# Moving one modulation group and issuing attention's value products in a row, in a two-layer hybrid diffusion backbone

## The chip, the cores and the metric

The kernel runs on one core of a Trainium2 chip. A core has five engines that run at once and are tied together by semaphores: TensorE (PE: matrix products; PEld is its weight loads), VectorE (DVE), ScalarE (ACT), GpSimd (POOL) and SyncE (SP), which here issues all the loads and stores. The metric is the device time of one execution in microseconds (us), as the median of several runs.

## The reference, cut to what matters

Two layers work on 512 latent and 256 context tokens of width 1024, in float32. Each layer has a mixer and a convolutional gated network (ConvFFN); in front of both stands an RMS norm whose scale and shift come from a conditioning vector, and behind both a gate from the same vector:

```python
def adaln_mods(cond, p):
    return jnp.split(jax.nn.silu(cond) @ p['ada_w'] + p['ada_b'], 6, axis=-1)

def trunk_layer(x_lat, x_ctx, c, c_ctx, p, mixer, rope, need_ctx):
    m_lat = [m[:, None, :] for m in adaln_mods(c, p)]
    m_ctx = adaln_mods(c_ctx, p)
    o_ctx, o_lat = mixer(modulate(x_ctx, p['norm_mix_g'], m_ctx[0], m_ctx[1]),
                         modulate(x_lat, p['norm_mix_g'], m_lat[0], m_lat[1]), p, rope, need_ctx)
    x_lat = x_lat + m_lat[2] * o_lat
    x_lat = x_lat + m_lat[5] * conv_ffn(modulate(x_lat, p['norm_ffn_g'], m_lat[3], m_lat[4]), p)
    ...
```

So a layer has six modulation groups of 1024 numbers for each of the two conditioning vectors: 0 and 1 are shift and scale of the mixer's norm, 2 its gate, 3 and 4 shift and scale of the network's norm, 5 the network's gate. Layer 1 needs the context's modulation for groups 0 and 1 only, since its context output is not used further.

Layer 0's mixer is latent attention beside RWKV-7 heads (a recurrence in chunks); layer 1's is Mamba-2 beside windowed attention. The windowed attention has 8 query heads in 2 groups; each block of 128 queries sees the 256 context keys and up to three blocks of 128 latent keys:

```python
s_win = jnp.where(mask, s_win, -jnp.inf)
p = sink_softmax(jnp.concatenate([s_ctx, s_win], axis=-1), sink).astype(v.dtype)
return (jnp.einsum('bghqk,bkgd->bqghd', p[..., :n_ctx], v_ctx)
        + jnp.einsum('bghqk,bkgd->bqghd', p[..., n_ctx:], vw))
```

## The kernel before, in words

Activations lie with the channels on the partitions, 128 at a time, and the tokens along the free dimension. Large products split weights and activations into a high and a low part in a reduced-width float (`whi`, `wlo`) and make three passes over them (`dense`, L367). `load_w` (L322) loads a weight, ScalarE makes the high part (L327), VectorE or GpSimd the low one (L328). All products go through the helper `mm` (L263), so they carry its line, L269, in the profile and are told apart by their tiles.

The order on each engine comes from a planner: it takes the instructions in the order of the program, simulates their times, and issues on each engine the earliest one of the program that is ready by its estimate. `tc.issue_after(ins)` puts what its block issues behind `ins` on the same engine. At run time each engine keeps its fixed order.

**Modulation.** A group is worked out in one of two ways.

- `ada_group` (L393), on TensorE: eight loads of 128 x 1024 weights (tile `aw`, 512 KB each), and for each four products `128*32 128x256` into four partition strips of one PSUM bank; a copy on VectorE (L406, `am`), two transposes (L409), and one addition of the bias that writes the group's columns of the tile `mods0` or `mods1` (L411).
- `ada_rows` (L415), on VectorE: the weights come transposed (`ada1t`), 128 outputs at a time, and one multiply with a running sum (L426) gives 128 outputs from a 128 x 1024 tile. It is a generator; each `next` makes one row. In the kernel before, it makes 16 rows for the context vector (groups 0 and 1 of layer 1) and 24 for the latent one (groups 0 to 2), 40 in all, and adds the bias at the end of each vector (L428).

Where the groups stand before: layer 0's groups 1 and 0 at the start (L520); layer 0's groups 2 to 5 in the mixer, one behind each of the four head pairs (p = 0 to 3) of the RWKV part (L802), with two weight buffers; layer 1's group 3 at the norm of layer 0's network, as the `fill` of `prenorm` (L1211), where TensorE waits for the norm; layer 1's rows during layer 0's network, two after each step j from 1 on (L1170); layer 1's group 4 behind layer 1's first norm (L1220) and group 5 in the fill at layer 1's network (L1630). In a fill, `paced` (L471) holds the products behind the last product before it.

**RWKV part of the mixer.** For each p, `features` (L613) projects and prepares, `rwkv_prep` (L716) makes the chunk products (`gk`), and `rwkv_inverse` (L755) inverts small triangular matrices, mostly on GpSimd (L765, L767), with transposes on VectorE (L759, L772 to L775) and products `iv`; its results go to memory and come back for the recurrence.

**Network.** `ffn` (L1130) takes 22 steps j in four groups (6, 6, 5, 5 steps in layer 0). A step makes two `up` products, each followed by a convolution (ScalarE L382, VectorE L383 and L385), a gate (L1163, L1164) and a split (L389, L390); behind each group come eight `down` products, each added to the residual with gate 5 (`resid`, L501). The rows are pinned behind the split's last instruction (`dve_last`).

**Windowed attention.** `swa_max` (L1481) works out the maxima of the scores of one query block, `swa_block` (L1516) its attention; block i + 1's maxima stand ahead of block i's attention in the program. In `swa_block`, for each block of 128 keys (4, 5, 5 and 4 of them for the four query blocks): for each of the 2 groups two score products and where needed a mask product into a PSUM tile `ab` (three buffers), one exponential on ScalarE (L1535) into `pt` (four buffers); then one value product for each group (L1538), `128*64 128x512`, group 0 into partitions 0 to 63 and group 1 into 64 to 127 of the tile `o`:

```python
            for g in range(2):
                mm(o[H[g]], lhsT=vv[:, tb * P + 64 * g:tb * P + 64 * g + 64], rhs=pts[g], start=n == 0,
                   stop=n == len(tbs) - 1)
```

GpSimd sums the exponentials (L1544). The output projection (`wo<-go`, from the Mamba part) needs none of this and is issued in between; the attention's part of it (`wo<-sh`, `wo<-sl`) follows.

Of the kernel before, what the change touches and what calls it, by code (L numbers as in the profile page):

```python
# [17 lines left out]
P = 128  # L18
D = 1024
# [3 lines left out]
NTOK = NCTX + NLAT  # L23
# [14 lines left out]
NAW = 2  # L38
# [90 lines left out]
def layout(inp):  # L129
    g = {k: np.asarray(v) for k, v in inp.items()}  # L130
    a = {}
    xt = np.concatenate([g["ctx"][0], g["x"][0]], 0).T
    a["xT"] = xt.reshape(KT, P, NTOK).transpose(1, 0, 2)
    cc = np.stack([g["c"][0], g["c_ctx"]], 1)
    a["cc"] = cc.reshape(KT, P, 2).transpose(1, 0, 2)
    a["ada"] = g["ada_w"].reshape(2, KT, P, 6, 1024).transpose(0, 3, 1, 2, 4)
    a["ada1t"] = g["ada_w"][1][:, :3 * D].T.reshape(24, P, D)
    a["ccrow"] = np.stack([g["c"][0], g["c_ctx"]], 0)
    ab = g["ab_w_in"][0]
    krs = np.concatenate([ab[:, 656:672], ab[:, 640:656]], 1)  # L140
    rw = ab[:, 672:]
    z64 = np.zeros((D, 64), np.float32)
    tiles = [rw[:, 1536:1600], ab[:, 640:672], krs, z64, rw[:, 1600:1664], rw[:, 1664:1792]]
    for p in range(4):
        for b in range(3):
            tiles.append(rw[:, b * 512 + p * P: b * 512 + (p + 1) * P])
    tiles.append(ab[:, :640])
    a["w_in"] = pack_w(np.concatenate(tiles, 1))
    qu = g["mla_w_q_up"][0].reshape(384, 8, 96)
    qu = np.concatenate([qu, qu[:, :, 80:96], qu[:, :, 64:80]], 2).reshape(384, 1024)  # L150
    a["w_q"] = pack_w(qu)
    kv = g["mla_w_kv_up"][0].reshape(256, 8, 128)
    a["w_k"] = pack_w(np.ascontiguousarray(kv[:, :, :64]).reshape(256, 512))
    a["w_v"] = np.ascontiguousarray(kv[:, :, 64:]).reshape(2, P, 4, P).transpose(1, 0, 2, 3).reshape(P, 8, P)
    a["w_out"] = pack_w(g["ab_w_out"][0])
    a["up"] = np.stack([pack_w(g["ffn_w_up"][i]) for i in range(2)])
    a["down"] = np.stack([pack_w(g["ffn_w_down"][i]) for i in range(2)])
    a["lora"] = np.concatenate([g["rwkv_w2"][0], g["rwkv_a2"][0]], 1).transpose(1, 0, 2)
    a["g2"] = g["rwkv_g2"][0]
    pv = {}  # L160
    for i in range(2):
        pv[f"ada_b{i}"] = g["ada_b"][i]
        pv[f"norm_mix_g{i}"] = g["norm_mix_g"][i]
        pv[f"norm_ffn_g{i}"] = g["norm_ffn_g"][i]
        for t in range(3):
            pv[f"conv_w{i}{t}"] = g["ffn_conv_w"][i, t]
        pv[f"conv_b{i}"] = g["ffn_conv_b"][i]
        pv[f"w0_{i}"] = g["rwkv_w0"][0, i]
        pv[f"a0_{i}"] = g["rwkv_a0"][0, i]
    pv["final_norm_g"] = g["final_norm_g"]  # L170
    pv["qn_g"], pv["kvn_g"] = g["mla_q_norm_g"][0], g["mla_kv_norm_g"][0]
    for n in ("mu_prev", "mu_next"):
        m = g["rwkv_" + n][0]
        z = np.zeros((64,), np.float32)
        q = [m[1536:1600], z, z, m[1600:1664], m[1664:1792]]
        for p in range(4):
            for b in range(3):
                q.append(m[b * 512 + p * P: b * 512 + (p + 1) * P])
        pv[n] = np.concatenate(q)
    for n in ("k_k", "k_a", "ln_g", "ln_b"):  # L180
        pv[n] = g["rwkv_" + n][0]
    pv["r_k"] = g["rwkv_r_k"][0].reshape(-1)
    for t in range(5):
        pv[f"sconv_w{t}"] = g["ssm_conv_w"][0, t]
    pv["sconv_b"] = g["ssm_conv_b"][0]
    pv["ssm_norm_g"] = g["ssm_norm_g"][0]
    pv["ssm_dx"] = np.repeat(g["ssm_d"][0], 64)
    z16 = np.zeros((16,), np.float32)
    for n in ("dt_bias", "a_log"):
        m = g["ssm_" + n][0]  # L190
        pv[n] = np.concatenate([m[0], z16, m[1], z16, np.zeros((64,), np.float32)])
    cd = g["cd_w_in"][0]
    zc, xc, dc, qc, kc, vc = np.split(cd, [1024, 2560, 2592, 3104, 3232], 1)
    qc = qc.reshape(D, 2, 4, 64).transpose(0, 2, 1, 3).reshape(D, 512)
    zp = np.zeros((D, 16), np.float32)
    dc = np.concatenate([dc[:, :16], zp, dc[:, 16:], zp, np.zeros((D, 64), np.float32)], 1)
    a["w_in1"] = pack_w(np.concatenate([xc, dc, zc, qc, kc, vc], 1))
    wo = g["cd_w_out"][0]
    wa = wo[1024:].reshape(2, 4, 64, D).transpose(1, 0, 2, 3).reshape(512, D)
    a["w_out1"] = pack_w(np.concatenate([wo[:1024], wa], 0))  # L200
    a["rows"] = g["swa_sink"][0].reshape(2, 4).T.reshape(1, 8)
    a["pv"] = np.concatenate([cols(np.asarray(pv[n], np.float32)) for n, _ in PV_SPEC], 1)
    cs = consts()
    a["const"] = np.concatenate([cs[n] for n, _ in CONST_ORDER], 1)
    a["scanm"] = cs["scanm"]
    a["scan2"] = cs["scan2"]
    a["const1"] = np.concatenate([cs["le"], cs["ge"]], 1)
    a["rope_a"], a["rope_c"], a["rope_s"] = rope_const()
    return {k: np.ascontiguousarray(v, dtype=np.float32) for k, v in a.items()}
# [3 lines left out]
def hybrid_kernel(ctx: ExitStack, tc: tile.TileContext, a, out):  # L213
# [201 lines left out]
    def ada_rows(mods, pool, bufs):  # L415

        for c in (1, 0):
            sr = T(pool, [P, D], "srow", 1)
            dma(sr, a["ccrow"][c:c + 1].partition_broadcast(P))
            act(sr, sr, AF.Silu)  # L420
            nt = 16 if c else 24
            for n in range(nt):
                w = T(pool, [P, D], "aw", bufs)
                dma(w, a["ada1t"][n])
                with tc.issue_after(dve_last[0]):
                    stt(out=w, in0=w, scalar=1.0, in1=sr, op0=ALU.mult, op1=ALU.mult, accum_out=mods[:, n, c:c + 1])  # L426
                yield
            tt(out=mods[:, :nt, c], in0=mods[:, :nt, c], in1=pv[:, PV["ada_b1"]:PV["ada_b1"] + nt], op=ALU.add)  # L428
# [367 lines left out]
    for p in range(4):  # L796
        fe = features(p)
        cur = rwkv_prep(p, *fe)
        if pend:
            rwkv_inverse(p - 1, *pend)  # L800
        pend = cur
        ada_group(0, p + 2, mods0, "pj", NAW)  # L802
    rwkv_inverse(3, *pend)
    close_pool("pp", "pa", "pj", "iv", "gk", "bkp")

# [166 lines left out]
    for tb in range(6):  # L972
        b = bank()
        n = 0
# [155 lines left out]
    def ffn(layer, mods, xs, segs, width, side, fill, nsegs=None, r=None, beside=None):  # L1130
# [13 lines left out]
        for gsz in FG[layer]:  # L1144
            us, ul = [], []
            halves = layer and j0 + gsz == FT
            for j in range(j0, j0 + gsz):
                cv = []
                for jj in (j, FT + j):
                    ps = acc()  # L1150
                    dense(ps, next_w("up"), P, hh, hl, segs=segs, by_pass=j < 2)
                    o = S()
                    conv3(o, ps, ALL, col(f"conv_w{layer}0", jj), col(f"conv_w{layer}1", jj), col(f"conv_w{layer}2", jj),
                          col(f"conv_b{layer}", jj), segs)
                    cv.append(o)
                    if halves:
                        raw = T("sb", [P, 8, P], "wraw", NWR)
                        dma(raw[:, :gsz], a["down"][layer, len(wb)][:, j0:])
                        hi, lo = [T("hold", [P, 4, P], "w", 16, F32R) for _ in range(2)]
                        split(hi, lo, raw[:, :gsz])  # L1160
                        wb.append((hi, lo))
                gt, vl = cv
                act(gt[:, n0:], gt[:, n0:], AF.Silu)  # L1163
                tt(out=vl[:, n0:], in0=gt[:, n0:], in1=vl[:, n0:], op=ALU.mult)  # L1164
                hi, lo = S(F32R), S(F32R)
                split(hi[:, n0:], lo[:, n0:], vl[:, n0:])
                us.append(hi)
                ul.append(lo)
                if beside is not None and j > 0:
                    next(beside, None)  # L1170
                    next(beside, None)
            if halves:
                break
            for m in range(8):
                ps = acc()
                dense(ps, next_w("down"), P, us, ul, nk=gsz, segs=segs)
                resid(xs[m], ps, mods, 5, m, segs)
            j0 += gsz
# [29 lines left out]
        close_pool("ffn")  # L1208

    open_pool("aw2", "right")  # L1210
    ffn(0, mods0, xs, SEG2, NTOK, "left", lambda: ada_group(1, 3, mods1, "aw2", 4),  # L1211
        beside=ada_rows(mods1, "aw2", 4))


# [301 lines left out]
    def swa_block(i, es):  # L1516
# [5 lines left out]
        for n, tb in enumerate(tbs):  # L1522
# [3 lines left out]
            for g in range(2):  # L1526
# [7 lines left out]
                pt = T("at2", [P, 512], "pt", 4)  # L1534
                act(pt, ps, AF.Exp)  # L1535
                pts.append(pt)
            for g in range(2):
                mm(o[H[g]], lhsT=vv[:, tb * P + 64 * g:tb * P + 64 * g + 64], rhs=pts[g], start=n == 0,  # L1538
                   stop=n == len(tbs) - 1)
            for g in range(2) if n < len(tbs) - (i == 3) else ():  # L1540
                if n == 0:
                    first[g] = pts[g]
# [105 lines left out]
```

## Time and profile before

| | |
|---|---|
| median of 3 runs | 2253.11 us (2247.74 to 2253.65) |
| the profiled execution | 2259.24 us, its span 2257.2 us, mean TensorE clock 0.955 |
| layer 0's mixer, up to the output projection | 0 to 732 us |
| output projection and norm | 732 to 821 us |
| layer 0's network | 821 to 1370 us |
| layer 1's mixer | 1370 to 1866 us, windowed attention from about 1700 on |
| layer 1's network | 1866 to 2257 us |
| modulation products: in the mixer's loop | 108 to 371 us |
| modulation products: fill at layer 0's network | 806 to 821 us |
| rows on VectorE (L426) | 40, from 854 to 1320 us |

How to read it. A line of the timeline has the start, the duration, the engine, the line, the operation, `output<-inputs`, the shape and a count of merged instructions; brackets hold the engine's idle time before it and what ended it. A float32 product with 128 x 512 moving elements takes two passes and shows as two records. A row of the table by stretch has, for each engine, its busy time and instruction count, then the granted TensorE clock (1.00 is full), the busy share of the DMA engines and GB/s. A line of the groups has the busy time and the mean duration in ns, then the idle time before. The chain that ended last is followed back from the last instruction, at each step to what released it.

### The profile page before, as it was taken

What the parts mean: (1) busy time and instruction counts of PE and PEld (TensorE: products, weight loads), DVE (VectorE), ACT (ScalarE), POOL (GpSimd) and SP (SyncE); (2) the same over time, 40 slices, a digit from 0 to 9 for tenths busy, and PEclk for the clock granted to TensorE, in tenths of its full rate; (3) what the DMA queues carried; (4) which work ended last, traced back from release to release, by engine and by line L of the source; (5) the groups of instructions that cost most, each with busy time, mean ns of one, the idle gap of its engine ahead of it and who ended that gap; (6) DMA issues with size and microseconds to landing.
All of it is one profiled execution on the core that took longest, in us unless ns stands there. A gap on an engine that the chain in (4) does not pass through costs nothing.

```text
span 2257.2 us, 33584 instructions
## 1 busy us (share of the span) xinstructions
PE 2066.3 (92%) x13360; PEld 1636.3 (72%) x13360; DVE 1393.8 (62%) x2157; ACT 930.8 (41%) x1437; POOL 506.2 (22%) x486
## 2 busy tenths in 40 slices
PE   5888989788998999999999999898878999999997
PEld 3666667576654878888888886776665667888886
DVE  5566865666877466456465554678984556554555
ACT  4445663532355253233132335644353345332434
POOL 0027686521233100000000014433631330000000
PEclk9989999698999999999999999998999999999998
DMA  8477777669521443333233333213426032323231
GB/s 300 121 202 197 192 204 192 213 175 294 168 96 54 152 140 114 102 103 119 87 115 101 103 112 117 90 47 117 133 85 159 28 126 71 94 89 98 84 117 61
DMA packets 183660, 292.00 MB, mean 129 GB/s; under 512 B 63616, under 2 KB 118944, under 8 KB 180432
## 3 DMA queue, kind: packets, MB, share of 16 engines
q1 hardware_dynamic: 183504, 289.86, 41.8%
q8 instruction: 105, 1.72, 0.3%
q14 instruction: 51, 0.42, 0.1%
HBM read 234.87 MB, written 47.33 MB: 125 GB/s over the span
## 4 chain that ended last, share of the span: by engine, by line
PE 64%; DVE 7%; ACT 5%; DMA 4%; issue 3%; POOL 1%; SPq 1%; DVEq 0%; ACTq 0%; POOLq 0%
PE acc L269 50%; PE sd L269 3%; PE b L269 3%; PE o L269 2%; PE ab L269 2%; PE wo L269 2%; DVE E L1376 2%; DMA E<-sp_ac 1%; PE ax L269 1%; POOL I L767 1%; DMA rec<-sp_rec 1%; POOL w L765 1%; ACT L433 0%; PE iv L269 0%; PE gk L269 0%
## 5 line engine op out<-in xcount | busy, mean ns | idle before, releaser
L269 PE MATMUL acc<-s,whi 128*128 128x512 f32 (+1 forms) x3104 | 766.6, 358 | 1.6 <-ACT s L480 1.6
L269 PEld LDWEIGHTS acc<-s,whi 128*128 128x128 f32 x3104 | 546.2, 188 | 93.9 <-ACT s L480 5.5
L269 PE MATMUL acc<-s,wlo 128*128 128x512 f32 (+1 forms) x1552 | 456.4, 354 | 0.0
L269 PE MATMUL acc<-h,whi 128*128 128x256 f32 (+2 forms) x1248 | 318.9, 369 | 18.6 <-DVE f L385 8.0
L327 ACT CAST whi<-wraw 128x1024 fp32r<-128x1024 f32 (+5 forms) x228 | 210.2, 923 | 278.3 <-PE acc L269 202.9
L269 PEld LDWEIGHTS acc<-s,wlo 128*128 128x128 f32 x1552 | 289.9, 188 | 47.1 <-DVE wlo L328 0.7
L269 PEld LDWEIGHTS acc<-h,whi 128*128 128x128 f32 (+1 forms) x1248 | 221.0, 195 | 71.4 <-issue 15.2
L328 DVE TENSOR_TENSOR wlo<-wraw,whi 128x1024 fp32r<-128x1024 f32 (+5 forms) x205 | 218.6, 1070 | 45.6 <-ACT whi L327 45.0
L383 DVE SCALAR_TENSOR_TENSOR s<-acc,pv,s 128x511 f32<-128x511 f32 (+1 forms) x132 | 87.0, 659 | 204.4 <-ACT s L382 204.0
L382 ACT ACTIVATE s<-acc,pv 128x512 f32<-128x512 f32 (+1 forms) x132 | 93.3, 707 | 234.8 <-PE acc L269 198.9
L501 DVE SCALAR_TENSOR_TENSOR x<-acc,mods,x 128x512 f32<-128x512 f32 (+1 forms) x136 | 79.4, 620 | 172.2 <-PE acc L269 172.1
L269 PE MATMUL acc<-h,wlo 128*128 128x256 f32 (+2 forms) x624 | 178.4, 360 | 0.0
L451 POOL TENSOR_TENSOR f<-f,f 128x768 f32<-128x768 f32 (+1 forms) x24 | 31.4, 1308 | 632.9 <-ACT f L446 623.0
L269 PEld LDWEIGHTS acc<-h,wlo 128*128 128x128 f32 (+1 forms) x624 | 118.4, 193 | 21.8 <-issue 5.5
L1194 POOL TENSOR_TENSOR s<-w,s 128x256 f32<-128x256 f32 x6 | 5.0, 861 | 382.9 <-ACT s L433 382.9
L385 DVE SCALAR_TENSOR_TENSOR s<-acc,pv,s 128x511 f32<-128x511 f32 (+1 forms) x132 | 87.0, 659 | 3.7
L767 POOL TENSOR_TENSOR I<-I,w 128x30 f32<-128x30 f32 (+14 forms) x120 | 77.4, 645 | 9.0
L765 POOL TENSOR_TENSOR w<-I 128x30 f32<-128x30 f32 (+14 forms) x120 | 68.9, 574 | 34.9 <-PE iv L269 26.0
L328 POOL TENSOR_TENSOR wlo<-wraw,whi 128x1024 fp32r<-128x1024 f32 x23 | 62.9, 2735 | 58.1 <-ACT whi L327 54.6
L389 ACT CAST s<-s 128x768 fp32r<-128x768 f32 (+1 forms) x44 | 32.0, 728 | 106.0 <-DVE s L1164 105.9
L1376 DVE TENSOR_SCALAR E<-E,acm 128x128 f32<-128x128 f32 x128 | 61.2, 547 | 15.0 <-ACT G L1373 15.0
L740 DVE TENSOR_TENSOR W<-gk,con 64x512 f32<-64x512 f32 x48 | 32.8, 683 | 53.5 <-ACT PB L739 50.7
(389 smaller groups left out, 3390.1 us busy)
## 6 DMA issues: line engine op xcount, KB each, us to landing
wraw<-up SPq DMA_DIRECT2D x88, 512.0 KB, 3.5
aw<-ada SPq DMA_DIRECT2D x72, 512.0 KB, 5.7
rec<-sp_rec SPq DMA_DIRECT2D x24, 1024.0 KB, 7.5
wraw<-w_in SPq DMA_DIRECT2D x47, 512.0 KB, 3.6
aw<-ada1t SPq DMA_DIRECT2D x40, 512.0 KB, 4.3
wraw<-down SPq DMA_DIRECT2D x40, 384.0 KB, 3.2
sp_rec<-tg SPq DMA_DIRECT2D x24, 384.0 KB, 3.2
E<-sp_ac SPq DMA_DIRECT2D x16, 512.0 KB, 6.1
```

Source lines behind the costliest of these rows:

```text
L269: ins = nc.tensor.matmul(o, lhsT=lhsT, rhs=rhs, start=start, stop=stop, skip_group_check=shared)
L327: nc.scalar.copy(hi[:, :kt], raw[:, :kt])
L328: (eng or tt)(out=lo[:, :kt], in0=raw[:, :kt], in1=hi[:, :kt].bitcast(F32), op=ALU.subtract)
L382: act(o[rows, t0:t0 + n], ps[rows, po:po + n], AF.Identity, scale=w1, bias=b)
L383: stt(out=o[rows, t0 + 1:t0 + n], in0=ps[rows, po:po + n - 1], scalar=w0, in1=o[rows, t0 + 1:t0 + n], op0=ALU.mult, op1=ALU.add)
L385: stt(out=o[rows, t0:t0 + n - 1], in0=ps[rows, po + 1:po + n], scalar=w2, in1=o[rows, t0:t0 + n - 1], op0=ALU.mult, op1=ALU.add)
L389: nc.scalar.copy(hi, src)
L501: stt(out=x[:, t0:t0 + n], in0=ps[:, po:po + n], scalar=mods[:, c6 * 8 + m, c:c + 1], in1=x[:, t0:t0 + n], op0=ALU.mult, op1=ALU.add)
L740: tt(out=w[hk], in0=b[hk].rearrange("p c (a t) -> p c a t", a=2), in1=mk[hk].rearrange("p (a t) -> p a t", a=2).unsqueeze(1).to_broadcast( ...
L765: eng.tensor_tensor(out=tmp, in0=I[:, m + 1:, m:m + 1].to_broadcast([P, n, m]), in1=I[:, m:m + 1, :m].to_broadcast([P, n, m]), op=ALU.mult)
L767: eng.tensor_tensor(out=I[:, m + 1:, :m], in0=I[:, m + 1:, :m], in1=tmp, op=ALU.add)
L1376: ts(out=e[:, h], in0=e[:, h], scalar1=acm[:, c, h0 + h:h0 + h + 1], scalar2=0.0, op0=ALU.subtract, op1=ALU.min)
```

## The change

Three things are changed.

- Layer 0's group 5, the last one in the mixer's loop (p = 3), is taken out there and becomes the fill at the norm of layer 0's network, in place of layer 1's group 3.
- Layer 1's group 3 goes to the rows on VectorE: the latent vector gets 32 rows in place of 24 (48 in all), the transposed weights grow to four groups, and the steps j of layer 0's network make two and three rows in turn (three in odd steps) in place of two.
- In the windowed attention, group 1's value product is issued first, and group 0's is put behind it with `issue_after`.

```diff
-    a["ada1t"] = g["ada_w"][1][:, :3 * D].T.reshape(24, P, D)
+    a["ada1t"] = g["ada_w"][1][:, :4 * D].T.reshape(32, P, D)
@@ ada_rows
-            nt = 16 if c else 24
+            nt = 16 if c else 32
@@ the loop over p in layer 0's mixer
         pend = cur
-        ada_group(0, p + 2, mods0, "pj", NAW)
+        if p < 3:
+            ada_group(0, p + 2, mods0, "pj", NAW)
     rwkv_inverse(3, *pend)
@@ ffn
                 if beside is not None and j > 0:
-                    next(beside, None)
-                    next(beside, None)
+                    for _ in range(2 + j % 2):
+                        next(beside, None)
@@
-    ffn(0, mods0, xs, SEG2, NTOK, "left", lambda: ada_group(1, 3, mods1, "aw2", 4),
+    ffn(0, mods0, xs, SEG2, NTOK, "left", lambda: ada_group(0, 5, mods0, "aw2", 4),
         beside=ada_rows(mods1, "aw2", 4))
@@ swa_block
-            for g in range(2):
-                mm(o[H[g]], lhsT=vv[:, tb * P + 64 * g:tb * P + 64 * g + 64], rhs=pts[g], start=n == 0,
-                   stop=n == len(tbs) - 1)
+
+            for g in (1, 0):
+                with tc.issue_after(pe_last[0]) if g == 0 else nullcontext():
+                    mm(o[H[g]], lhsT=vv[:, tb * P + 64 * g:tb * P + 64 * g + 64], rhs=pts[g], start=n == 0,
+                       stop=n == len(tbs) - 1)
```

## The prediction

> **What bounds the kernel now.** I read the page first, for who is busy and who ends last.
>
> ```profile
> PE 2066.3 (92%) x13360; PEld 1636.3 (72%) x13360; DVE 1393.8 (62%) x2157; ACT 930.8 (41%) x1437; POOL 506.2 (22%) x486
> PE 64%; DVE 7%; ACT 5%; DMA 4%; issue 3%; POOL 1%; SPq 1%; DVEq 0%; ACTq 0%; POOLq 0%
> ```
>
> TensorE is busy in 92% of the span and carries 64% of the chain that ended last; no other engine has over 7% of it. So an edit is worth what it takes from TensorE where TensorE is full, and the next view is the busy time by stretch, for the places that the change touches: layer 1's window attention, the end of layer 0's mixer, layer 0's network, and one stretch that waits for loads.
>
> ```profile
> core 0: us, PE busy (x) PEld busy (x) DVE busy (x) ACT busy (x) POOL busy (x), PEclk, DMA share, GB/s
> 1734.00:1846.00 112.00, 111.44 (x485) 68.16 (x484) 56.96 (x80) 43.98 (x87) 38.04 (x30) 1.00 0.17 56
> 350.00:400.00 50.00, 49.71 (x443) 40.50 (x438) 22.40 (x29) 19.91 (x45) 34.75 (x60) 0.93 0.69 178
> 822.00:1370.00 548.00, 547.81 (x3120) 479.81 (x3119) 306.50 (x450) 168.88 (x217) 16.15 (x8) 1.00 0.33 105
> 1700.00:1720.00 20.00, 14.71 (x53) 10.11 (x54) 14.19 (x26) 8.51 (x12) 0.00 (x0) 0.79 1.08 269
> ```
>
> In the window attention TensorE works 111.44 of 112.00 us while VectorE has half of the time free (56.96), ScalarE and GpSimd more. In layer 0's network it works 547.81 of 548.00, and VectorE 306.50. So work taken from TensorE in the first row is time, and work given to VectorE in the third has room.
>
> **Part 1, the value products in a row: the main term.** The timeline of TensorE shows what a product of one group costs alone and beside the other. A product's two passes are two records, so x2 is one product, x4 a product of each group.
>
> ```profile
> 1734.26 0.22 PE L269 MATMUL sd<-mle,identr 128*128 128x128 f32 x1
> 1734.32 0.28 PE L269 MATMUL sd<-mge,identr 128*128 128x128 f32 x1
> 1734.53 1.08 PE L269 MATMUL o<-pt,vv 128*64 128x512 f32 x4
> 1735.54 0.50 PE L269 MATMUL ab<-qa,ka 128*128 128x512 f32 x1
> ...
> 1743.31 0.40 PE L269 MATMUL ab<-qb,kb 65*128 65x512 f32 x1
> 1743.55 0.40 PE L269 MATMUL ab<-mle,identr 128*128 128x512 f32 x1
> 1743.88 1.07 PE L269 MATMUL o<-pt,vv 128*64 128x512 f32 x2
> 1744.89 0.50 PE L269 MATMUL ab<-qa,ka 128*128 128x512 f32 x1
> ...
> 1833.49 1.94 PE L269 MATMUL o<-pt,vv 128*64 128x512 f32 x8
> ```
>
> Alone: from the score product before it (1743.55) to the next (1744.89) are 1.34 us; a score product by itself takes 0.24 (1743.31 to 1743.55), so 1.10 are the value product's. Both groups together: 1734.32 to 1735.54 are 1.22, less about 0.06 to 0.11 for the small mask product (1734.26 to 1734.32 is 0.06), so 1.11 to 1.16. The two groups write different halves of the output's partitions, and side by side they take the time of one. A pair made out of two lone products saves 2 x 1.10 - 1.13 = 1.07 us.
>
> How many are alone? The group of lines has all of them:
>
> ```profile
> L269 PE MATMUL o<-pt,vv 128*64 128x512 f32 x72 | 34.1, 615 | 0.0
> ```
>
> 72 records are 36 products. In the timeline I find x4 twice and x8 once, that is 8 products in 4 pairs, so 28 are alone; 28 x 1.07 + 2 x 1.08 + 1.94 = 34.06, the group's busy time. So 14 pairs are to be had: 14 x 1.07 = 15.0 us of TensorE. I do not take all. `issue_after` puts group 0's product behind group 1's but does not forbid another between them, and the maxima of the next block stand earlier in the program than this block's values; I let 2 of 14 break: 12 x 1.07 = 12.8. And one wait is added: group 0's product used to run during group 1's exponential and is now queued behind a product that needs it. On TensorE everything behind it is held too: the next scores, the maxima, the output projection.
>
> ```profile
> 1744.05 0.60 ACT L1535 ACTIVATE pt<-ab 128x512 f32<-128x512 f32 x1 [1.32 <-PE ab L269]
> ```
>
> This is the exponential of the scores that end with the product at 1743.55. They have streamed in by 1743.79, the exponential is over at 1744.65, so a value product directly behind its scores would wait 0.86 us. Today scores of the next keys and the output projection stand between; they are still there, so most of the wait stays covered. I take 0.8 us in all, one uncovered wait. Were none covered, 18 pairs x 0.86 = 15.5 us would eat the gain. Group 0's exponentials keep their buffer longer, but four buffers hold two key blocks, and GpSimd's sums hold them already. Value: -12.0, bounds -15.0 and +0.5.
>
> At this place a page speaks against the change. The Trainium skill, "TensorE: Matmul & The Clock Gate", "Part 3: Packing small matmuls", says that a weight load overlaps matmuls in flight only when the row groups differ; both value products use all 128 rows, so by it the second would wait, this part would bring nothing, and the sum below would be -2.1 in place of -14.1. The row with x4 in 1.08 us does not agree, and the row decides. What no row shows for certain is group 1 ahead of group 0, as the change has it.
>
> **Part 2, one modulation group less in the mixer.** The group's products in its stretch and, from the chain of waits, those that lie on the chain:
>
> ```profile
> L269 PE MATMUL bkp<-aw,sc 128*32 128x256 f32 x64 | 5.4, 449 | 1.5 <-ACT p L625 1.5
> ```
>
> ```profile
> 351.97 1.86 PE bkp L269 x16
> ...
> 364.02 0.57 PE bkp L269 x8
> ...
> 367.25 0.57 PE bkp L269 x8
> ...
> 370.92 0.37 PE bkp L409 x2
> ```
>
> 32 of the 64 records (16 + 8 + 8) and the two transposes are on the chain: 1.86 + 0.57 + 0.57 + 0.37 = 3.37 us, in a stretch where TensorE works 49.71 of 50.00. The other 32 records fill TensorE before that, while other engines lead the chain, and cost nothing. What comes next is not TensorE alone:
>
> ```profile
> 399.30 0.54 DVE L328 TENSOR_TENSOR wlo<-wraw,whi 128x256 fp32r<-128x256 f32 x1 [4.18 <-ACT whi L327]
> 406.53 0.68 POOL L892 MEMSET u<- 64x256 f32 x2 [4.55 <-PE gk L269]
> 409.59 1.90 DVE L772 STREAM_TRANSPOSE PN<-I 128x1024 f32<-128x1024 f32 x1
> 420.79 0.25 POOL L765 TENSOR_TENSOR w<-I 128x30 f32<-128x30 f32 x1 [13.36 <-PE iv L269]
> ```
>
> VectorE at 399.30 waits (through ScalarE) for a projection of TensorE, GpSimd's memset at 406.53 for TensorE's last products of the group p = 3, the transpose at 409.59 for another memset behind that one, and the last inverse, at 420.79, for the products that follow the transposes. So an earlier TensorE is passed on, less what loads in between hold. I take 2.4 of 3.37. The order in this stretch is made anew by the planner, so the bounds are -5.4 (all of the group) and +4.6 (a queue slip of the size of GpSimd's 4.55). The group's eight loads leave SP's queue here too.
>
> **Part 3, the fill changes its group: nothing.** Layer 0's last group takes the place, the pool and the eight loads of layer 1's group 3, with the same products behind the same pin. Its result came late before as well:
>
> ```profile
> 826.70 0.17 DVE L411 TENSOR_TENSOR mods<-b,pv 128x16 f32<-128x16 f32 x1
> ...
> 926.40 1.14 DVE L501 SCALAR_TENSOR_TENSOR x<-acc,mods,x 128x256 f32<-128x256 f32 x2 [2.41 <-PE acc L269]
> ```
>
> The first user of group 5 is the residual at 926.40, nearly 100 us later. A new risk: the fill now writes the tile that the norm reads. Layer 1's network does just that already:
>
> ```profile
> 1869.44 4.88 ACT L480 ACTIVATE s<-s,mods 128x256 fp32r<-128x256 f32 x12
> ...
> 1882.95 0.17 DVE L411 TENSOR_TENSOR mods<-acc,pv 128x16 f32<-128x16 f32 x1 [3.06 <-PE acc L409]
> ```
>
> ScalarE reads its columns 13 us before the fill writes its own, so there is no such wait.
>
> **Part 4, eight more rows on VectorE.** They come in odd steps j, a third row behind two.
>
> ```profile
> 870.41 0.96 DVE L390 TENSOR_TENSOR s<-s,s 128x768 fp32r<-128x768 f32 x1 [0.96 <-ACT s L389]
> 871.29 1.22 DVE L426 SCALAR_TENSOR_TENSOR aw<-aw,srow 128x1024 f32<-128x1024 f32 x1
> 872.43 0.08 DVE L426 DVE_READ_ACCUMULATOR aw<-aw,srow 128x1 f32 x1
> ...
> 876.68 0.75 DVE L383 SCALAR_TENSOR_TENSOR s<-acc,pv,s 128x511 f32<-128x511 f32 x1 [0.85 <-ACT s L382]
> ...
> 881.71 0.48 DVE L383 SCALAR_TENSOR_TENSOR s<-acc,pv,s 128x255 f32<-128x255 f32 x1 [3.49 <-ACT s L382]
> ...
> 888.14 1.22 DVE L426 SCALAR_TENSOR_TENSOR aw<-aw,srow 128x1024 f32<-128x1024 f32 x1
> ```
>
> A row costs 1.14 us (871.29 to 872.43). A step lasts 16.85 (871.29 to 888.14), and VectorE waits in it 0.96 + 0.85 + 3.49 = 5.30: the third row fits and leaves 4.2. What stands behind it, the convolution of the next tile and a weight's low part, is 1.14 later in a queue that then waits for TensorE anyway. Cover gone, 8 x 1.14 = 9.1 us. The eight more loads go to a stretch where the DMA engines are 0.33 busy; SP holds the weights' loads behind them until a row's buffer is free. I take +0.3.
>
> **The sum.** -12.0 - 2.4 + 0.0 + 0.3 = -14.1. The profiled execution took 2259.24 us (span 2257.2 and 2.0 around it), 6.1 above the median of 2253.11; the stages above are that run's, and the difference carries over: 2253.1 - 14.1 = 2239.0.
>
> **Rivals.**
> A, the pairs do not run side by side (group 1 first is different, or others get between as a rule): parts 2 and 4 are left, -2.1, so 2251.0. For it: the unseen order; against: four pairs in the trace. 0.09. By the page's rule of part 1 this would be the outcome.
> B, the mixer's new order slips by the 4.6 while the pairs come: -12.0 + 4.6 + 0.3 = -7.1, so 2246.0. For it: GpSimd's 13.36 us wait shows how loosely that stretch hangs together. 0.13.
> C, all of it: 14 pairs and the whole group, -15.0 - 5.4 = -20.4, so 2232.7. 0.08.
> D, slower: TensorE waits at every pair for group 1's exponential, and the granted clock falls with the waits. In the row of 1700 to 1720, where it works 14.71 of 20 us, the clock is 0.79, in the attention 1.00. Then 111.4 - 15.0 = 96.4 of work at 0.79 are 122.0, with 15.5 of waits 137.5 against 112, +25.5, and with parts 2 and 4 +23.4: 2276.5. It decides from a busy share of about 0.74 (14.71 of 20), and 96.4 of work beside 15.5 of waits is 0.86 even with no wait covered. 0.03. The Trainium skill ("TensorE: Matmul & The Clock Gate", Part 1) has the clock fall after an idle window of about 3.4 us; by it waits of 0.86 would not do it.
>
> **The numbers.** Forecast 0.67 at 2239.0 (about 2234 to 2245 with its own bounds), A 0.09, B 0.13, C 0.08, D 0.03. 0.3%, about what a measurement of this kernel can tell from no change, is 6.8 us: faster is below 2246.3. That is the forecast but for 0.03, C, and half of B: 0.64 + 0.08 + 0.06 = 0.78; the same 0.03 + 0.07 + 0.09 = 0.19; slower D, 0.03. The range leaves out A, D, and the far end of C: 2232 to 2248.
>
> **What would show it.** The mixer of layer 0 ends, in the chain of waits of before, where the output projection begins:
>
> ```profile
> 732.06 67.93 PE acc L269 x384
> ```
>
> In the profile after this should stand 1 to 5 us earlier. `o<-pt,vv` should have x4 in nearly all places and a busy time near 34.1 - 12.8 = 21 us, with TensorE as full as before and the attention some 12 us shorter; 48 rows at the row line, and layer 0's network within 1 us of its 548. Wrong would be: x2 records with other products between (A), a mixer that ends later (B), waits of TensorE for `pt` with a PEclk below 1.0 (D), or a TensorE that waits for `wlo` in layer 0's network (part 4).

## The result, and the profile after

| | before | after |
|---|---|---|
| median | 2253.38 us (2247.74 to 2254.56, 4 runs) | 2236.78 us (2236.03 to 2239.12, 4 runs) |
| profiled execution, its span | 2259.24, 2257.2 us | 2239.12, 2237.4 us |

The ratio is 0.9929 (95% interval 0.9912 to 0.9947): 16.0 us faster, 11.9 to 19.8 by the interval. The forecast was 14.1 us and 2239.0. In what follows a ratio to before is turned into microseconds with 2253.4.

The page of after has TensorE's busy time down by 25.3 us with 66 records fewer, and its share of the chain about where it was:

```profile
PE 2041.0 (91%) x13294; PEld 1637.5 (73%) x13294; DVE 1401.0 (63%) x2171; ACT 931.3 (42%) x1437; POOL 504.8 (23%) x486
PE 63%; DVE 6%; ACT 5%; DMA 3%; issue 3%; POOL 1%; SPq 1%; DVEq 0%; ACTq 0%; POOLq 0%
```

In the groups of lines, the three that the change touches:

```profile
L269 PE MATMUL o<-pt,vv 128*64 128x512 f32 x72 | 19.0, 615 | 0.0
L269 PE MATMUL bkp<-aw,sc 128*32 128x256 f32 x320 | 28.4, 433 | 25.2 <-DMA aw<-ada 24.8 <-DVE mods L411 0.3
L426 DVE SCALAR_TENSOR_TENSOR aw<-aw,srow 128x1024 f32<-128x1024 f32 x48 | 56.5, 1220 | 0.7 <-ACT srow L420 0.7
```

The value products are the same 72 records and take 19.0 us where they took 34.1. One group (64 records) has left the mixer. The rows are 48, each as long as before.

The timeline of TensorE shows one pair before its neighbour, and near the end two pairs in a row:

```profile
1756.23 1.08 PE L269 MATMUL o<-pt,vv 128*64 128x512 f32 x4
1757.24 0.50 PE L269 MATMUL ab<-qa,ka 128*128 128x512 f32 x1
...
1817.27 1.94 PE L269 MATMUL o<-pt,vv 128*64 128x512 f32 x8
```

Two products, four records, 1.08 us: the same as in the pairs that the kernel before had already, though group 1 now stands first. There are fourteen x4 and two x8, so all 18 pairs stand together.

Where the stages end is read from the chain of waits (start, length). First before, then after; the first line of each is layer 0's network, the last is layer 1's:

```profile
821.41 548.41 PE acc L269 x3123
...
1882.91 350.11 PE acc L269 x1563
```

```profile
728.29 66.56 PE acc L269 x378
...
816.92 548.41 PE acc L269 x3123
...
1859.13 354.69 PE acc L269 x1586
```

Layer 0's mixer ends at 728.29 in place of 732.06, 3.8 earlier. The network takes 548.41 in both. From its end to the end of layer 1's network it was 863.20 (1369.82 to 2233.02), now 848.49 (1365.33 to 2213.82): 14.7 less. In these two profiles 3.8 + 14.7 = 18.5 of the 19.8 between the spans lie in these two places, and the last 1.3 elsewhere. The 14.7 hold up below; the 3.8 are within what a mixer differs by from profile to profile.

### The profile page after: what moved, and what is told of

Its sections match the earlier page's. It is cut to its first block, busy times and chain, and to the rows that moved or that the text cites. A ratio compares the mean times of both kernels' runs of the same rounds, so it can differ in the third digit from the quotient of the medians.

```text
span 2237.4 us, 33443 instructions
## 1 busy us (share of the span) xinstructions
PE 2041.0 (91%) x13294; PEld 1637.5 (73%) x13294; DVE 1401.0 (63%) x2171; ACT 931.3 (42%) x1437; POOL 504.8 (23%) x486
## 4 chain that ended last, share of the span: by engine, by line
PE 63%; DVE 6%; ACT 5%; DMA 3%; issue 3%; POOL 1%; SPq 1%; DVEq 0%; ACTq 0%; POOLq 0%
PE acc L269 49%; PE sd L269 3%; PE b L269 3%; PE wo L269 3%; PE ab L269 2%; PE o L269 2%; DVE E L1377 1%; DMA E<-sp_ac 1%; DMA f<-sp_k 1%; PE ax L269 1%; POOL I L767 1%; POOL w L765 1%; ACT L433 0%; DMA rec<-sp_rec 0%; DMA xtm<-f 0%
## 5 line engine op out<-in xcount | busy, mean ns | idle before, releaser
L385 DVE SCALAR_TENSOR_TENSOR s<-acc,pv,s 128x511 f32<-128x511 f32 (+1 forms) x132 | 87.1, 660 | 3.7
L765 POOL TENSOR_TENSOR w<-I 128x30 f32<-128x30 f32 (+14 forms) x120 | 70.0, 584 | 34.1 <-PE iv L269 14.0
```

What stands on the lines that cost most here:

```text
L385: stt(out=o[rows, t0:t0 + n - 1], in0=ps[rows, po + 1:po + n], scalar=w2, in1=o[rows, t0:t0 + n - 1], op0=ALU.mult, op1=ALU.add)
L765: eng.tensor_tensor(out=tmp, in0=I[:, m + 1:, m:m + 1].to_broadcast([P, n, m]), in1=I[:, m:m + 1, :m].to_broadcast([P, n, m]), op=ALU.mult)
```

## The experiments

The twelve runs fall into four questions. Times are medians; each ratio is to before on the same chip. After itself, measured again under other names, gives the base for all that is added to it: 0.9929 as after, 0.9934 as the third run below.

**What each part is worth.** The first run has the value products in a row and nothing else of the change; its edit against before:

```diff
-            for g in range(2):
-                mm(o[H[g]], ...)
+            for g in (1, 0):
+                with tc.issue_after(pe_last[0]) if g == 0 else nullcontext():
+                    mm(o[H[g]], ...)
```

> The kernel before with the new order of the value products alone. Theory (the pairs carry the gain): all 18 pairs stand together, the value products' busy time falls from 34.1 to 19.0 us as in the kernel after, and 12 to 15 us of the time go: ratio 0.9933 to 0.9945 to the kernel before. Rival (the profiled execution of before was 6 us above its median, so a part of what the two profiles differ by was its own, and the pairs' 15 us of TensorE are partly given back to waits): 6 to 10 us, ratio 0.9955 to 0.9975. The mixer of layer 0 ends at 732 us as before, within 1 us, in both.

Measured: 2240.64 us, ratio 0.9937 (0.9921 to 0.9953), so 14.2 us faster (10.6 to 17.8). Its chain of waits:

```profile
726.03 67.78 PE acc L269 x384
...
815.61 548.41 PE acc L269 x3123
...
1858.30 355.42 PE acc L269 x1586
```

From network end to network end 849.70 (1364.02 to 2213.72), 13.5 less than before, and `o<-pt,vv` is 19.0 us busy. This is the main term, and it stands by itself. The first line is a warning, and there my expectation failed (732, within 1): TensorE's order is before's up to the attention, and yet the mixer ends at 726.03 in place of 732.06. One profile does not tell a mixer's end to better than some 6 us.

The second run has the moved group and the rows, with the old value products; its edit against after, as those that follow unless another kernel is named:

```diff
-            for g in (1, 0):
-                with tc.issue_after(pe_last[0]) if g == 0 else nullcontext():
-                    mm(o[H[g]], ...)
+            for g in range(2):
+                mm(o[H[g]], ...)
```

> The kernel after with the value products in their old order: the moved group and the eight more rows alone. Theory: the mixer of layer 0 ends some 3.8 us before 732, the rest is as before, and 2.5 to 5 us go: ratio 0.9978 to 0.9989. Rival (the mixer's shorter time is only that of one execution, or the planner's luck): within 1.5 us of before, 0.9993 to 1.0007. Rival two (the rows cost VectorE's cover): slower than before, layer 0's network over 549 us.

Measured: 2250.11 us, ratio 0.9980 (0.9968 to 0.9991), so 4.5 us faster (2.0 to 7.2). Its networks in the chain of waits:

```profile
811.65 548.41 PE acc L269 x3123
...
1866.54 355.05 PE acc L269 x1586
```

From network end (1360.06) to network end (2221.59) it is 861.53, within 1.7 of before. The two parts add up to 18.7, after has 16.0, and the intervals hold both.

**What makes the pairs.** Is it the pin, the order, or the different halves of the output? The third run drops the pin:

```diff
             for g in (1, 0):
-                with tc.issue_after(pe_last[0]) if g == 0 else nullcontext():
+                with nullcontext():
                     mm(o[H[g]], ...)
```

> The kernel after with group 1's product first in the program but without the pin that holds group 0's behind it. Theory (without the pin the planner issues group 0's product as soon as its own exponential is done, in the time in which group 1's runs): most products are alone again, x2 records in more than 20 places, value products busy 30 to 34 us, and the time is that of the move alone, 2249 to 2251. Rival (the order in the program is enough): 15 or more pairs, busy 19 to 22 us, and 2237 as after.

Measured: 2240.06 us, ratio 0.9934 (0.9917 to 0.9951). What I expected did not come: the planner gives the same instructions in the same order on all five engines, with the pin or without it, so this is after once more. The pin does nothing. The other way round, group 0 first and group 1 pinned behind it, the planner gives all five engines the order of the second run, with its lone products; that version was not run on the chip. So the order in the program is what counts here. That agrees with the planner's rule, though no run takes the reason apart: group 1's exponential comes last, and when group 1's product is issued, group 0's, which writes the same tile behind it, has nothing else to wait for. With group 0 first, its product is ready early and is issued alone.

The next run keeps the row and takes the halves away: group 1's products also write partitions 0 to 63, except for the last key block of each query block. Group 1's part of the attention output then holds that last key block alone, and the values of its others are added into group 0's.

```diff
-                    mm(o[H[g]], ..., start=n == 0, stop=n == len(tbs) - 1)
+                    last = n == len(tbs) - 1
+                    mm(o[H[g if last else 0]], ..., start=g == 1 and (n == 0 or last), stop=last)
```

> After, but group 1's value products write partitions 0 to 63 as group 0's do, except at each query block's last key block (so group 1's part of the attention output holds its last key block alone): 14 of the 18 pairs then stand in a row, or nearly so, on the same half. Theory H (a pair is cheap because the two products have different halves and run side by side): each of the 14 costs its full two, 0.85 to 1.07 us more, the value products' busy time goes from 19.0 to 31 to 34 us, the time to 2249 to 2252. Rival R (it is the row that saves, whichever half: no other shape in between): busy time 19 to 22 us, the time within 3 us of after's 2236.8.

Measured: 2248.44 us, ratio 0.9975 (0.9964 to 0.9987), 10 us slower than after. Its group of lines, and a pair in its timeline:

```profile
L269 PE MATMUL o<-pt,vv 128*64 128x512 f32 x72 | 32.0, 606 | 0.0
```

```profile
1756.85 1.93 PE L269 MATMUL o<-pt,vv 128*64 128x512 f32 x4
1758.71 0.50 PE L269 MATMUL ab<-qa,ka 128*128 128x512 f32 x1
```

The same four records in a row take 1.93 us on one half and 1.08 on two, and the busy time is up by 13.0. So theory H holds: in a row on one half the products run one after the other, on two halves side by side. The row alone saves little: 1.93 against 2 x 1.07 for two lone products. One thing stays open: with the half, the two products also share the places that they add into, and the run does not tell these two apart. The time of 2248.4 falls 0.6 short of the 2249 that I gave as the lower end.

**What the moved group costs where it was.** Three runs put pieces of it back into after at p = 3, where the group itself stays in the fill; their results go nowhere.

```diff
         if p < 3:
             ada_group(0, p + 2, mods0, "pj", NAW)
+        else:
+            w = T("pj", [P, 1024], "aw", NAW)
+            dma(w, a["ada"][0, 5, 0])
+            am = T("pj", [P, 256], "am", 1)
+            for _ in range(3):
+                b = bank()
+                for k in range(KT):
+                    for g in range(4):
+                        mm(b[32 * g:32 * g + 32, :256], lhsT=sc[:, k], rhs=w[:, 256 * g:256 * g + 256], ...)
+                nc.vector.tensor_copy(am, b[:, :256])
+                for q in range(2):
+                    nc.tensor.transpose(b[:, 256 + q * P:256 + (q + 1) * P], am[:, q * P:(q + 1) * P], ident)
+                nc.vector.tensor_copy(am[:, 0:16], b[:, 256:272])
```

This is the run with the products, three times over. The two with loads have in its place:

```diff
+            b = bank()
+            am = T("pj", [P, 64], "am", 1)
+            for k in range(2 * KT):
+                w = T("pj", [P, 1024], "aw", NAW)
+                dma(w, a["ada"][k // KT, 5, k % KT])
+                mm(b[0:32, :64], lhsT=sc[:, k % KT], rhs=w[:, 0:64], ...)
+            nc.vector.tensor_copy(am[0:32], b[0:32, :64])
```

with `range(KT)` and group 5's first eight tiles, `a["ada"][0, 5, k]`, in the smaller one.

> After, with the moved group's products back in the mixer at p = 3, three times over and on one loaded tile (their result goes nowhere; the group itself stays in the fill). It asks what a group's work on TensorE costs there, at three times its size. Theory P (TensorE sets the pace of that stretch, a group costs the 2.4 to 3.4 us that the prediction took): 7 to 10 us above after, 2244 to 2247. Rival L (the move's 4.5 us are the loads', the products lie in waits): within 2 us of after, 2236 to 2239.

Measured: 2250.78 us, ratio 0.9982 (0.9972 to 0.9993): some 11 us above after, 3.8 for a group, a little more than the 7 to 10 of theory P. Not all of it is TensorE's: in the groups of lines from 300 to 400 us a memset on GpSimd waits 10.5 us for the copies on VectorE, which stand behind the added products. After has 1.0 there; first after, then this run:

```profile
L718 POOL MEMSET LS<- 128x256 f32 x1 | 0.3, 317 | 1.0 <-DVE I L759 1.0
L718 POOL MEMSET LS<- 128x256 f32 x1 | 0.3, 317 | 10.5 <-DVE am L817 10.5
```

> After, with loads of the moved group's kind back in the mixer at p = 3, sixteen in place of eight, each read by one product of 64 columns that TensorE runs in order as it did the group's (the results go nowhere). It asks what the loads alone cost, at twice their size. Rival L (the loads hold up SP's queue or TensorE, as in the 5.03 us that TensorE waited for one of them at 139 in before; they make the 4.5 of the move): about 9 us above after, 2245 to 2248. Theory P: 0 to 2 above after, 2237 to 2239. If neither this run nor the one with products is above after by more than 3, the move's 4.5 us are not its own cost in the mixer and its cause stays open.

Measured: 2253.49 us, ratio 0.9998 (0.9985 to 1.0011): 15 us above after, more than rival L had.

> After, with eight such loads back in the mixer at p = 3 (as many as the moved group had), each read by one product of 64 columns; the results go nowhere. The run with sixteen was 0.68% (15 us) slower than after, more than three times the move's own 4.5. Theory X (the first eight cost what the move saved, the loads alone account for it): 4 to 5 us above after's 2236.8 to 2240, about 0.995 of before. Rival Y (each eight cost the same 7.7): 0.9965. Rival Z (the stretch has room for the first eight, and only the second eight overfill it): within 2 us of after, 0.9930 to 0.9940.

Measured: 2238.64 us, ratio 0.9932 (0.9919 to 0.9946): after's own time to within some 3 us, so rival Z. Eight loads with their readers, as many as the moved group had, show no cost there; sixteen cost 15 us. In the profile with sixteen the mixer ends at 737.81 (after's at 728.29). But the planner's order changes with them: from trace to trace, TensorE's order differs from after's in some 80 places with sixteen loads and in some 25 with eight, so the 15 us need not be the transfers'. What they are is open. The same holds for the run with the products, whose order differs in some 100 places, and for the change itself: before's order and after's differ in some 100 places up to the output projection. So the loads are unlikely to be what the move saved; its gain in the mixer may be the products', what is queued behind them, or the new order, and the runs do not tell these apart.

That the move gains is shown by the timed runs (0.9980). Single profiles don't show it: in profiles whose TensorE order is the same up to there, the output projection begins at scattered times. Here are two with and without the group, the first run of the next part and the same-half run, and then the latest and the earliest without it, from the runs with two and three more multiplies at the end, which change nothing ahead of layer 0's network.

```profile
729.82 68.27 PE acc L269 x384
```

```profile
724.87 66.58 PE acc L269 x378
```

```profile
732.90 66.57 PE acc L269 x378
```

```profile
722.28 66.55 PE acc L269 x378
```

With the group: 732.06, 726.03 and 729.82, mean 729.3. Without: 728.29, 724.51 (second run), 727.25 (third run), 724.87, 728.24 and 728.18 (group 4 as rows, one more multiply), 732.90 and 722.28, mean 727.1. That is 2.2 less, with a spread of 6.0 and 10.6 for the same order.

**What the fill and the rows cost.** One run is before with group 3 as rows (transposed weights, `nt` and rows per step as in after) and nothing in the fill; group 5 stays in the mixer. The fill's edit against before:

```diff
-    ffn(0, mods0, xs, SEG2, NTOK, "left", lambda: ada_group(1, 3, mods1, "aw2", 4),
+    ffn(0, mods0, xs, SEG2, NTOK, "left", None,
```

> Before, with layer 1's group 3 made as rows (48 rows, two and three per step) and nothing in the fill at the norm of layer 0's network; layer 0's group 5 stays in the mixer, the value products stay as before. It asks what the fill and the eight more rows cost by themselves. Theory F (both are free): within 2 us of before's 2253.4, the network at 548.4 us. Rival G (the fill's products hold TensorE back at the end of the norm): 1 to 4 us faster, 2249 to 2252. Rival K (the products keep the granted clock up over the norm's wait, without them the network begins slower): 2 to 5 us slower, 2255 to 2258, the network's 548.4 longer or PEclk lower in the slice behind it.

Measured: 2254.25 us, ratio 0.9996 (0.9986 to 1.0005). Theory F, for the sum of fill and rows. The stretch from 806 to 817 us by engine, first after and then this run, shows that something does change under it:

```profile
806.00:817.00 11.00, 11.00 (x70) 7.93 (x70) 9.19 (x19) 6.36 (x13) 0.00 (x0) 0.90 0.67 241
```

```profile
806.00:817.00 11.00, 9.15 (x40) 7.86 (x41) 10.23 (x20) 9.38 (x17) 0.00 (x0) 0.69 0.00 0
```

Without the fill TensorE has 30 records fewer in these 11 us, and a granted clock of 0.69 in place of 0.90. The last piece of its network in the chain of waits:

```profile
836.18 531.13 PE acc L269 x3024
```

From the mixer's end to the network's end it is 637.49 us (729.82 to 1367.31) against 637.04 in after. So in the time as a whole the fill does not delay the network, and leaving it empty gains nothing. Whether what rival G would gain and what rival K would lose cancel, the run does not tell.

The next run gives VectorE eight rows more: layer 1's group 4, from the place behind layer 1's first norm, as rows too, three in every step.

```diff
-    a["ada1t"] = g["ada_w"][1][:, :4 * D].T.reshape(32, P, D)
+    a["ada1t"] = g["ada_w"][1][:, :5 * D].T.reshape(40, P, D)
-            nt = 16 if c else 32
+            nt = 16 if c else 40
-                    for _ in range(2 + j % 2):
+                    for _ in range(3):
-    ada_group(1, 4, mods1, "aw2", 4, late=True)
+    nc.gpsimd.memset(mods1[:, 32:40, 1:2], 0.0)  # at the start
```

> The kernel after, and layer 1's group 4 too as rows on VectorE (56 rows, three in each step), nothing of it left at layer 1's first norm; its context half, which nothing uses, is set to zero. Theory A (TensorE's 8 x 0.57 us of that group at the norm lie on the path there): 3 to 5 us less than after, 2232 to 2234. Theory B (TensorE waits there for the low parts that VectorE makes, 0.3 us at 1390, so the products fill time that is lost anyway): 0 to 1.5 us less than after. In both layer 0's network stays at 548 us: its third row in even steps too is covered; if the cover ends, it grows by up to 8 x 1.14 = 9 us.

Measured: 2241.79 us, ratio 0.9935 (0.9913 to 0.9957), no different from after; the network still takes 548.42. The rows are free once more. That fits theory B, by which the group was free where it stood, but the interval is 4 us wide on either side and does not rule out the lower end of theory A. And one thing else has changed: here one of the 18 pairs is broken, although the pin is there, and the value products take 1.5 us more.

```profile
L269 PE MATMUL o<-pt,vv 128*64 128x512 f32 x72 | 20.5, 618 | 0.0
```

Where does the cover end? Three runs put K = 1, 2 and 3 further multiplies of the same size behind every row in `ada_rows`:

```diff
+                    for _ in range(K):
+                        tt(out=w, in0=sr, in1=sr, op=ALU.mult)
```

> After, with one more 128 x 1024 multiply on VectorE behind each of the 48 rows, pinned like the row (about 1.1 us each; its result goes nowhere). It asks where VectorE's cover in layer 0's network ends: in before VectorE waits 5.30 us in a step of 16.85, and made two rows of 1.14 in it, so rows have 7.6 us per step. Here a step takes 2 x 2.24 = 4.5 or 3 x 2.24 = 6.7 us of row work. Theory S (the slack of the whole step counts): the network stays within 1 us of 548.4, the time within 2 us of after's. Rival E (a late row holds the convolution behind it and TensorE at once): the network is 5 to 20 us longer.

> After, with two more such multiplies behind each row. A step takes 6.7 or 10.0 us of row work in turn, 8.35 in the mean, against 7.6 us of room; the rows fill some 19 steps. Theory S with carry from step to step: 0.75 x 19 = 14 us longer. Theory S without carry (an odd step's excess of 2.4 is not made up in the next): 10 x 2.4 = 24 us longer. Rival E: more than 30 us longer.

> After, with three more such multiplies behind each row. A step takes 8.9 or 13.3 us of row work, 11.1 in the mean, 3.5 above the room: theory S gives 19 x 3.5 = 67 us longer. If the network is longer by much less, VectorE's waits as summed in one step (5.30) understate its room; if by much more, the rows' work is not only queued but delays TensorE's next product through a chain of its own.

Measured: 2238.71 us, ratio 0.9932 (0.9917 to 0.9947), with one; 2265.79 us, 1.0047 (1.0033 to 1.0061), with two; 2306.48 us, 1.0236 (1.0218 to 1.0253), with three. Against after that is 0, 26 and 69 us. The chain of waits of each, in the same order; with two and three the network is broken into pieces, of which the first and the last are shown:

```profile
815.32 548.47 PE acc L269 x3123
```

```profile
820.64 84.94 PE acc L269 x483
...
1342.07 50.81 PE acc L269 x288
```

```profile
809.70 51.24 PE acc L269 x291
...
1371.12 52.38 PE acc L269 x288
```

The network is 548.47, 572.24 (820.64 to 1392.88) and 613.80 (809.70 to 1423.50) long: 0, 24 and 65 more. Who held TensorE, in the waits of TensorE from 870 to 1400 us, with two and with three:

```profile
PE acc L269 <- DVE s L385: 17.9, 6, 6.7
```

```profile
PE acc L269 <- DVE s L385: 43.1, 8, 10.6
```

In after, and with one multiply, that line is not there. The convolution's second half (L385) is late, and TensorE stands. These waits are not all of the 24 and 65. TensorE's products take longer too, as the network's row in after and with three shows:

```profile
816.92:1365.33 548.41, 548.40 (x3123) 480.27 (x3122) 315.67 (x467) 168.68 (x216) 16.02 (x8) 1.00 0.34 113
809.70:1423.50 613.80, 563.87 (x3123) 490.04 (x3122) 470.45 (x611) 166.75 (x216) 16.03 (x8) 0.96 0.31 101
```

Of the 65.4, 49.9 are idle time of TensorE and 15.5 longer products, at a granted clock of 0.96 in place of 1.00. Theory S without carry gave 24 for two, and theory S 67 for three: the room of one step, 5.30 us of waits and the two rows that stood in it, fits all three runs, and the 14 of a carry from step to step does not fit the second.

## Why the prediction was right

*What bounds the kernel*: right. TensorE is nearly as full after as before where the change worked. By stretch, from the first value product to the end of the last, before and after:

```profile
1734.53:1843.78 109.25, 108.69 (x463) 65.63 (x462) 54.89 (x76) 43.55 (x86) 36.69 (x29) 1.00 0.17 56
1729.76:1824.79 95.03, 92.83 (x455) 64.58 (x454) 55.93 (x74) 42.49 (x84) 35.91 (x28) 0.98 0.21 64
```

The stretch is 14.2 us shorter: TensorE has 15.9 us less work in it and 1.6 more idle time. Of rival D, with waits at every pair and a clock at 0.79, there is little: one wait, and a clock of 0.98 where it was 1.00.

*Part 1, -12.0*: the mechanism was right, the size a little short. The runs give -14.2 (10.6 to 17.8 by the interval). The step that was off is "I let 2 of 14 break": in after none broke. By the planner's rule group 0's product is the earliest of the program that is ready when group 1's has been issued, so nothing comes between. (In the run with group 4 as rows one did break.) All 14 at 1.07 are 15.0, and the busy time fell by 15.1 (34.1 to 19.0); the 21 us that I looked for are 19.0. The added wait, 0.8 in the prediction, was 1.6, and another one than I meant: that a wait of about that size came at all is luck. The waits of TensorE from 1700 to 1850 us, before and after:

```profile
PE ab L269 <- ACT pt L1535: 0.6, 1, 0.6
```

```profile
PE ab L269 <- ACT pt L1536: 2.2, 1, 2.2
```

There is one wait for an exponential in both, 1.6 longer. It is not the value product's but a score product's, which waits for its buffer `ab`. Rival A is gone: group 1 first pairs as well as group 0 first.

The rule of the Trainium skill, "TensorE: Matmul & The Clock Gate", "Part 3: Packing small matmuls", that a weight load overlaps matmuls in flight only when the row groups differ, does not hold in these traces. Both products use all 128 rows, and here are the weight loads (PEld) of the pair in after, and of the pair on one half:

```profile
1756.23 0.20 PEld L269 LDWEIGHTS o<-pt,vv 128*64 128x64 f32 x4
```

```profile
1756.84 0.19 PEld L269 LDWEIGHTS o<-pt,vv 128*64 128x64 f32 x2
1757.33 0.14 PEld L269 LDWEIGHTS o<-pt,vv 128*64 128x64 f32 x1 [0.29 <-issue]
1757.76 0.14 PEld L269 LDWEIGHTS o<-pt,vv 128*64 128x64 f32 x1 [0.29 <-issue]
```

On two halves all four loads are over 0.20 us after the first product began, and the two products run until 1.08; on one half the third load starts 0.49 after the first. The rule is one of loads: that the second product itself would wait, and this part bring nothing, was the prediction's reading of it.

*Part 2, -2.4*: the run with the move alone gives -4.5 (2.0 to 7.2) for parts 2 to 4 together, against my -2.1. The size is inside the interval, barely. The means of the profiles say 2.2 earlier at the mixer's end, with a spread larger than that. Eight loads put back show no cost to within some 3 us (0.9932, after's ratio), and three groups of products put back cost 11 us, but in another order. So that the products are the cost, as the prediction had it, is likely and not shown; how much is TensorE's own time, how much the queue of VectorE and GpSimd behind it and how much the new order, the runs don't tell apart. Rival B, a mixer that slips by 4.6, did not come: it would have made the move alone some 5 us slower than before, and it is 4.5 faster.

*Part 3, 0*: right. In after's timeline the fill's group is ready nearly 100 us before its first user:

```profile
822.22 0.17 DVE L411 TENSOR_TENSOR mods<-b,pv 128x16 f32<-128x16 f32 x1
...
921.91 1.14 DVE L501 SCALAR_TENSOR_TENSOR x<-acc,mods,x 128x256 f32<-128x256 f32 x2 [1.25 <-PE acc L269]
```

The residual waits for TensorE (1.25), not for the group. Nor does the group wait for the norm that reads the same tile: its line at 822.22 has no wait.

*Part 4, +0.3*: right, and now with its limit. The network is 548.41 as it was, so even the 0.3 was not needed. One more multiply for each row is still free, two are not.

*The sum*: -14.1 against -16.0. Rival C, all of it with 2232.7, was nearer on Part 1 than the forecast was; on the whole the result lies between the two, closer to the forecast.

## What to carry to other kernels

Where two products write different halves of the partitions and each fills only half the array's columns, look at the timeline for whether they run together: here a lone one costs 1.10 us and a pair 1.13. If a planner issues what is ready first, write the one whose input comes last ahead of the other: here all 18 pairs held without a pin. Look again after any other change, since in one run a pair broke in spite of the pin. To judge what another engine can take on, sum its waits over one period of the loop and compare with the largest load in one period, not with the mean.

## What the runs showed of the hardware

- Two float32 products of 128 rows by 64 columns, 512 moving, take 1.08 us together on two halves of the output partitions, in either order of the halves, and 1.93 on one half.
- Eight loads of 512 KB more in the mixer cost nothing that shows (within some 3 us) and sixteen 15 us, with another order of the program beside it; the cause is open.
- With 30 records fewer in an 11 us stretch the granted clock was 0.69 in place of 0.90, and the network ended 637.49 us after the mixer, in place of 637.04.
- When VectorE kept TensorE waiting in layer 0's network (three more multiplies for each row), the granted clock was 0.96 in place of 1.00, and the same 3123 products took 563.87 us of busy time in place of 548.40.
- One stage repeats itself and another doesn't: with the same order on TensorE up to there, layer 0's mixer ended at 726.03, 729.82 and 732.06 in three profiles, and at 722.28 to 732.90 in the eight without the group, while the network took 548.41 to 548.47 wherever its chain of waits was in one piece. Why the mixer differs is not shown.
